# Seven-product units in two PSUM banks, with wider evictions and a moved first product

## The chip, the cores and the metric

The kernel runs on one core of a Trainium2 chip. The metric is the device time of one execution in microseconds (us); lower is better. TensorE is written PE, its weight loads PEld, VectorE DVE, ScalarE ACT, GpSimd POOL, and the queue that issues most of the DMAs SP.

## The reference, cut to what matters

The kernel computes a two-layer encoder for 512 tokens of width 1024. Each layer mixes retention and differential attention, and then adds a SwiGLU block. Only the last line of a layer is touched by the change:

```
for l in range(DEPTH):                       # 2
    ...
    x = x + jnp.concatenate([ret, da], axis=-1) @ w_out[l]
    h = rms_norm(x, ffn_norm_g[l])           # x: 512 x 1024
    x = x + (jax.nn.silu(h @ w_gate[l]) * (h @ w_up[l])) @ w_down[l]   # inner width 2816
```

## The kernel before, in words

Activations lie transposed: features on the 128 partitions, tokens along the free axis. A float32 product is made of three matmuls of a shortened format: each operand is split into a high part `hi` (a cast on ACT) and a rest `lo` (a subtraction on DVE), and hi\*hi, hi\*lo and lo\*hi are summed in PSUM.

The inner width of 2816 is 22 blocks of 128. The first 4 blocks go through ordinary products (`gate_up`). The other 18 use a seven-product scheme, one level of Strassen-Winograd: a "unit" takes the place of a 2x2 block product and makes seven products of half size instead of eight. There are 26 units in a layer: 18 for gate and up (n = 512, so that a product is 12 matmuls of 256 columns) and 2 x 4 for the way down (n = 384, 9 matmuls). I number them 0 to 25 in the order in which the program writes them: up units 0 to 5, up unit 6, down units 7 to 10, up units 11 to 15, up unit 16, down units 17 to 20, up units 21 to 25.

A unit is the generator `seven`. It loads four weight blocks (three DMAs on SP, and one on POOL that adds to what the first one brought), makes the sums of blocks that the scheme needs (L783, L785 on DVE), and splits three pairs of blocks into `hi` (L754, ACT) and `lo` (L755, DVE): pair a holds the weights of products b11 and t2, pair s31 those of t3 and t1, pair b those of b21 and t4; s4 is split alone for b22 (L748, L749). `hi` and `lo` have three buffers each (`NHL`), and a unit uses three, so pair a of a unit can be written only when the unit before has read its own pair a for the last time, in product t2. In the same way s31 waits for product t3 of the unit before, and pair b for t4.

The seven products go into PSUM. Four of them (b11, t2, t3, t4) pile up in one bank called `pa`, and the running sum is copied out between them: after b11 (L803), after t2 (L806) and after t3 (L809), on ACT each time, and after t4 inside `finish`. A product on `pa` has to wait until the copy ahead of it has read the bank. Product b21 has the bank `pb`, and t1 and b22 share the bank `pc`. The pools give two banks to each of the tags acc (for `pa`), sc (`pb`) and o (`pc`). What follows in `finish` is silu (L106, ACT), products on DVE, and the splits of the result for the way down.

The loop over the units sets the written order: `next(unit)`, `next(units[i + 1])`, `next(unit, None)`. So the loads, the splits and product b11 of the next unit stand where the second `yield` of a unit is. This is not yet the order on the engines: a scheduler that works on its own estimate of the times places each engine's instructions, mostly as written, but it lets later matmuls go ahead where it expects a wait. Each engine then runs its instructions strictly in that order and waits on semaphores.

Of the kernel before, what the change touches and what calls it, by code (L numbers as in the profile page):

```python
# [10 lines left out]
AF = mybir.ActivationFunctionType  # L11
ALU = mybir.AluOpType

P = 128
# [10 lines left out]
C = 256  # L25
# [29 lines left out]
def encoder_kernel(ctx: ExitStack, tc: tile.TileContext, xT, wfirst, wsingle, wvv, wout, wgu, wdn, wds, prm, lam, cst, outT):  # L55
    nc = tc.nc
# [10 lines left out]
    def nm(s):  # L67
        uid[0] += 1
        return f"{s}{uid[0]}"

    def big(s, dt=F32, tag="w", bufs=NW):
        return tpool.tile([P, T], dt, tag=tag, name=nm(s), bufs=bufs)
# [4 lines left out]
    def bank(tag, bufs):  # L77
        return psum.tile([P, 512], F32, tag=tag, name=nm(tag), bufs=bufs)

    acc_bank = lambda: bank("acc", 2)  # L80
    sc_bank = lambda: bank("sc", 2)
    out_bank = lambda: bank("o", 2)
# [98 lines left out]
    def pair():  # L181

        t = tpool.tile([P, 2, T], F32R, tag="h", name=nm("h"), bufs=8)
        return t[:, 0], t[:, 1]
# [25 lines left out]
    def cut(pair, *idx):  # L210
        return tuple(t[idx] for t in pair)
# [102 lines left out]
    def layer(l, n1, h, x_src, first_raw):  # L314
# [272 lines left out]
        q, k = [None] * 4, [None] * 4  # L587
# [50 lines left out]
        n2, h2, x = Norm(), [], []  # L638
# [73 lines left out]
        H1, H2 = slice(0, C), slice(C, T)  # L712
# [45 lines left out]
        def four(raw):  # L758
            return new_chunk(1024)[0] if raw else tpool.tile([P, 1024], F32, tag="ah", name=nm("s"), bufs=NAH)
# [3 lines left out]
        def seven(src, n, right, finish, by_load=True):  # L763


            A1, A2 = slice(0, n), slice(n, 2 * n)
            turns[0] += 1
            s31, a, b = (four(raw)[:, : 2 * n] for raw in (False, True, turns[0] % 2))
            s4 = big("s4")[:, :n]
            blocks = src.rearrange("p (i n) -> p i n", n=n)  # L770
            if by_load:
                sums = s31.rearrange("p (i n) -> p i n", n=n)
                nc.sync.dma_start(sums, blocks[:, 1:2].broadcast_to([P, 2, n]))
                nc.sync.dma_start(a[:, A1], blocks[:, 0])
                nc.sync.dma_start(b, src[:, 2 * n :])
                nc.gpsimd.dma_start(sums, blocks[:, 0::3], accum_op=ALU.add)  # L776
            else:
                nc.sync.dma_start(a, src[:, : 2 * n])
                nc.sync.dma_start(b, src[:, 2 * n :])
                i = nc.vector.tensor_tensor(s31[:, A2], a[:, A2], b[:, A2], op=ALU.add)  # L780
                tc.add_manual_dep(i.ins, last_split[0], order, reason="unit by unit")
                nc.vector.tensor_tensor(s31[:, A1], a[:, A2], a[:, A1], op=ALU.add)
            i = nc.vector.tensor_tensor(a[:, A2], a[:, A1], s31[:, A2], op=ALU.add)  # L783
            tc.add_manual_dep(i.ins, last_split[0], order, reason="unit by unit")
            nc.vector.tensor_tensor(s4, b[:, A1], a[:, A2], op=ALU.add)  # L785
            g1, s2 = split_in(a, n)
            first_cast[0] = last_cast[0]
            s3, s1 = split_in(s31, n)
            g2, u2 = split_in(b, n)
            s4 = cut(split_to(s4, [big("s4", F32R, "mix", NMIX)[:, :n] for _ in range(2)]), slice(None))  # L790

            pa, pb, pc = (bank() for bank in (acc_bank, sc_bank, out_bank))

            def product(ps, w, r, start):
                for k in range(n // P):
                    L, R = cut(w, slice(None), slice(k * P, (k + 1) * P)), right[k][r]
                    for i, (x1, x2) in enumerate(((0, 0), (0, 1), (1, 0))):
                        nc.tensor.matmul(ps[:, :C], L[x1], R[x2], start=start and k + i == 0, stop=k == n // P - 1 and i == 2, skip_group_check=True)  # L798


            g, u = big("g"), big("u")
            product(pa, g1, "b11", True)
            nc.scalar.copy(g[:, H1], pa[:, :C])  # L803
            yield
            product(pa, s2, "t2", False)
            nc.scalar.copy(g[:, H2], pa[:, :C])  # L806
            product(pc, s1, "t1", True)
            product(pa, s3, "t3", False)
            nc.scalar.activation(u[:, H2], pa[:, :C], AF.Copy, scale=-1.0)  # L809
            nc.vector.tensor_tensor(u[:, H2], u[:, H2], pc[:, :C], op=ALU.subtract)  # L810
            product(pb, g2, "b21", True)
            nc.vector.tensor_tensor(g[:, H1], pb[:, :C], g[:, H1], op=ALU.add)
            product(pa, u2, "t4", False)
            yield
            product(pc, s4, "b22", False)
            nc.vector.tensor_tensor(g[:, H2], pc[:, :C], g[:, H2], op=ALU.add)
            finish(g, u, pa[:, :C])

        def activation(act, j, pairs, wait):


            def finish(g, u, pa):
                tc.add_manual_dep(func(g, g, AF.Silu), first_cast[0], order, reason="the next unit first")
                if j < pairs:
                    u, half = big("u", tag="rn", bufs=4), u
                else:
                    half = u
                nc.vector.scalar_tensor_tensor(u[:, H1], pa, -1.0, g[:, H1], op0=ALU.mult, op1=ALU.mult)
                nc.vector.tensor_tensor(u[:, H2], half[:, H2], g[:, H2], op=ALU.mult)
                i = j % pairs  # L830
                spread = i == pairs - 1

                if j < pairs:
                    later.append(lambda: first_parts(u, spread))
                    if not (j == 0 and wait):
                        later.pop()()
                    return
                second_parts(u, act[i], spread)

            def first_parts(u, spread):  # L840
                t = big("b11", F32R, *(("rn", 4) if spread else ("w", NW)))
                t14 = pair()
                b11 = split_to(u[:, H1], (t[:, H1], t[:, H2]))
                nc.vector.tensor_tensor(u[:, H1], u[:, H1], u[:, H2], op=ALU.subtract)
                t1 = split_to(u[:, H1], cut(t14, slice(None), H1))
                act.append(dict(u=u, t14=t14, b11=b11, t1=t1))

            def second_parts(u, o, spread):
                v = o["u"]
                b2 = split_to(u, [big("b2", F32R, "mix", NMIX) for _ in range(2)] if spread else pair())  # L850
                nc.vector.scalar_tensor_tensor(v[:, H1], v[:, H1], -1.0, u[:, H2], op0=ALU.mult, op1=ALU.subtract)
                nc.vector.tensor_tensor(v[:, H2], u[:, H2], v[:, H2], op=ALU.subtract)
                t23 = split_to(v, pair())
                nc.vector.scalar_tensor_tensor(u[:, H1], v[:, H1], -1.0, u[:, H1], op0=ALU.mult, op1=ALU.subtract)
                t4 = split_to(u[:, H1], cut(o["t14"], slice(None), H2))
                for r, t, s in (("b21", b2, H1), ("b22", b2, H2), ("t2", t23, H1), ("t3", t23, H2)):
                    o[r] = cut(t, slice(None), s)
                o["t4"] = t4

            return finish  # L860

        def plain(act, j):
            def finish(g, u, pa):
                func(g, g, AF.Silu)
                nc.vector.scalar_tensor_tensor(u[:, H1], pa, -1.0, g[:, H1], op0=ALU.mult, op1=ALU.mult)
                nc.vector.tensor_tensor(u[:, H2], u[:, H2], g[:, H2], op=ALU.mult)
                act.append(split(u, *(("rn", 4) if j < 2 else ("h", 8))))

            return finish

        def down(m):
            def finish(g, u, pa):
                nc.vector.tensor_tensor(x[m], x[m], g, op=ALU.add)
                nc.vector.tensor_tensor(x[m + 4][:, H2], x[m + 4][:, H2], u[:, H2], op=ALU.add)
                nc.vector.tensor_tensor(x[m + 4][:, H1], x[m + 4][:, H1], pa, op=ALU.subtract)

            return finish

# [5 lines left out]
        act, n = [], a1 * P  # L884
# [4 lines left out]
        for m in range(KT):  # L889
# [6 lines left out]
            w = cut(ww, slice(None), slice(m % 2 * n, (m % 2 + 1) * n))  # L896
            ps = any_bank()
# [8 lines left out]
        for i, (a0, a1) in enumerate(FFN[1:]):  # L906
            act, half = [], (a1 - a0) // 2
# [20 lines left out]
        n, late = (a1 - a0) * P, []  # L928
        for m in range(KT):
            w = chunk(wdn[l, m][:, PLAIN * P :], n)  # L930
            if l + 1 == DEPTH and m == KT - 1:

                for t, queue in ((H1, nc.sync), (H2, nc.scalar)):
                    ps = any_bank()
# [5 lines left out]
            ps = any_bank()  # L940
# [17 lines left out]
    n, h, raws = Norm(), [], []  # L958
# [7 lines left out]
    for l in range(DEPTH):  # L966
        if l:
            raws = [load_chunk(wfirst[l, c]) for c in range(4)]
        n, h = layer(l, n, h, xT if l == 0 else xscr, raws)
# [94 lines left out]
```

## Time and profile before

| what | value |
| --- | --- |
| median of 3 runs | 1256.27 us (1254.27 to 1256.29) |
| span of the profiled execution, first to last instruction | 1252.7 us |
| what the median lies above that span | 3.6 us |
| granted TensorE clock | 1.000 |
| matmuls of the units (L798) | 4032 of 7954 |
| DVE busy, whole span | 1000.6 us (80%) |
| ACT busy, whole span | 724.5 us (58%) |

The page of the profile gives the span of the execution that was profiled; an own time of that execution beside it is not given, and the median of the runs is 3.6 us above the span. Matmuls are pipelined in the record: each is drawn 283 ns long, while the next one starts 120 ns later. So a PE that looks busy all the time may still lose time between the starts, and I read the starts. The two layers give nearly the same pattern, with the units from 339 to 598 us in the first and from 961 to 1220 us in the second.

### The profile page before, as it was taken

To read this page: it belongs to the slowest core of one execution; us is meant where nothing else is said; L and a number is where in the kernel's file an instruction comes from. 1 tells how busy PE (TensorE), PEld (TensorE's weight loads), DVE (VectorE), ACT (ScalarE), POOL (GpSimd) and SP (SyncE) were. 2 spreads that over 40 slices of the span, in tenths; PEclk is the share of its full clock that TensorE was granted. 3 is DMA by queue.
4 is the path that set the end of the run, shared out by engine and by line. 5 is a ranking of instruction groups with operands and counts; after the bars stand their busy time and mean duration, and the time that the engine had idled before them with its cause. 6 is when DMAs were issued, how large, how long until landed. Compare 5 with 4: busy or idle time off the path is not lost.

```text
span 1252.7 us, 20478 instructions
## 1 busy us (share of the span) xinstructions
PE 1235.7 (99%) x7954; PEld 1110.4 (89%) x7954; DVE 1000.6 (80%) x1742; ACT 724.5 (58%) x1230; POOL 80.7 (6%) x94
## 2 busy tenths in 40 slices
PE   9999999999999999999999999999999999999998
PEld 7888988788799999999888889987788999999997
DVE  6899769877978888886648997698779788888863
ACT  6778747455455555554538785564554565555541
POOL 1000000000011111110000000000100110110100
PEclk9999999999999999999999999999999999999999
DMA  7222213363176686683532122142632756866823
GB/s 260 84 68 68 68 67 120 100 151 101 54 171 156 155 220 158 156 220 89 170 104 85 51 84 68 51 151 76 159 101 64 179 148 170 211 150 169 207 69 101
DMA packets 67553, 157.81 MB, mean 126 GB/s; under 512 B 6144, under 2 KB 16640, under 8 KB 67456
## 3 DMA queue, kind: packets, MB, share of 16 engines
q1 hardware_dynamic: 52880, 130.90, 33.4%
q0 software_dynamic: 14144, 25.17, 12.0%
q8 instruction: 62, 1.02, 0.3%
q10 hardware_dynamic: 432, 0.44, 0.1%
q14 instruction: 35, 0.29, 0.1%
HBM read 152.29 MB, written 4.19 MB: 125 GB/s over the span
## 4 chain that ended last, share of the span: by engine, by line
PE 96%; DVE 2%; ACT 1%; DMA 0%; issue 0%; ACTq 0%
PE acc L798 22%; PE o L798 11%; PE acc L205 10%; PE acc L207 10%; PE acc L206 10%; PE sc L798 5%; PE o L205 3%; PE o L206 3%; PE o L207 3%; PE sc L205 3%; PE sc L207 3%; PE sc L206 3%; PE sc L404 2%; PE o L508 2%; PE sc L492 1%; PE aux L420 1%
## 5 line engine op out<-in xcount | busy, mean ns | idle before, releaser
L194 ACT CAST hi<-raw 128x1024 fp32r<-128x1024 f32 (+2 forms) x115 | 113.3, 992 | 122.3 <-PE sc L206 40.5
L198 DVE TENSOR_TENSOR lo<-raw,hi 128x1024 fp32r<-128x1024 f32 (+2 forms) x116 | 132.7, 1148 | 42.0 <-ACT hi L194 41.6
L205 PE MATMUL acc<-h,hi 128*128 128x512 f32 (+1 forms) x344 | 134.2, 392 | 1.1 <-ACT h L216 1.1
L207 PE MATMUL acc<-h,lo 128*128 128x512 f32 (+1 forms) x344 | 134.6, 391 | 0.0
L206 PE MATMUL acc<-h,hi 128*128 128x512 f32 (+1 forms) x344 | 134.5, 391 | 0.0
L798 PE MATMUL acc<-hi,hi 128*128 128x256 f32 x432 | 122.9, 284 | 0.0
L798 PE MATMUL acc<-hi,lo 128*128 128x256 f32 x432 | 122.2, 283 | 0.0
L798 PE MATMUL acc<-lo,hi 128*128 128x256 f32 x432 | 122.1, 283 | 0.0
L754 ACT CAST hi<-raw 128x1024 fp32r<-128x1024 f32 (+1 forms) x78 | 76.6, 982 | 76.4 <-PE acc L798 30.1
L754 ACT CAST hi<-s 128x1024 fp32r<-128x1024 f32 (+1 forms) x78 | 76.6, 982 | 62.2 <-issue 24.6
L755 DVE TENSOR_TENSOR lo<-s,hi 128x1024 fp32r<-128x1024 f32 (+1 forms) x78 | 89.0, 1141 | 20.9 <-ACT hi L754 20.4
L755 DVE TENSOR_TENSOR lo<-raw,hi 128x1024 fp32r<-128x1024 f32 (+1 forms) x78 | 88.9, 1140 | 20.7 <-ACT hi L754 20.6
L798 PEld LDWEIGHTS acc<-hi,hi 128*128 128x128 f32 x432 | 82.7, 191 | 0.4
L798 PEld LDWEIGHTS acc<-lo,hi 128*128 128x128 f32 x432 | 82.8, 192 | 0.2
L798 PEld LDWEIGHTS acc<-hi,lo 128*128 128x128 f32 x432 | 82.8, 192 | 0.0
L205 PEld LDWEIGHTS acc<-h,hi 128*128 128x128 f32 x344 | 64.6, 188 | 14.6 <-ACT h L216 1.3
L207 PEld LDWEIGHTS acc<-h,lo 128*128 128x128 f32 x344 | 64.6, 188 | 13.2 <-DVE lo L198 0.2
L206 PEld LDWEIGHTS acc<-h,hi 128*128 128x128 f32 x344 | 64.7, 188 | 12.8
L776 POOL DMA_DIRECT2D s<-in_wgu x36 | 43.5, 1208 | 445.6 <-DMA s<-in_wgu 262.7
L798 PE MATMUL o<-b,s 128*128 128x256 f32 x480 | 66.0, 283 | 0.0
L798 PEld LDWEIGHTS o<-b,s 128*128 128x128 f32 x480 | 61.4, 192 | 0.2
L106 ACT ACTIVATE sc<-sc,mx 128x512 f32<-128x512 f32 x64 | 46.0, 720 | 18.1 <-DVE mx L408 17.6
(267 smaller groups left out, 3709.5 us busy)
## 6 DMA issues: line engine op xcount, KB each, us to landing
s<-in_wgu SPq DMA_DIRECT2D x54, 512.0 KB, 5.9
s<-in_wgu POOLq DMA_DIRECT2D x36, 512.0 KB, 8.6
raw<-in_wgu SPq DMA_DIRECT2D x34, 512.0 KB, 4.8
raw<-in_wsingle SPq DMA_DIRECT2D x32, 512.0 KB, 3.7
raw<-in_wgu SPq DMA_DIRECT2D x36, 256.0 KB, 3.5
s<-in_wds SPq DMA_DIRECT2D x24, 384.0 KB, 3.6
raw<-in_wvv SPq DMA_DIRECT2D x16, 512.0 KB, 3.7
raw<-in_wout SPq DMA_DIRECT2D x16, 512.0 KB, 3.7
```

Source lines behind the costliest of these rows:

```text
L106: i = nc.scalar.activation(out, src, f, **kw).ins
L194: c = nc.scalar.copy(hi[:, s], raw[:, s])
L198: nc.vector.tensor_tensor(lo[:, s], raw[:, s], f32(hi[:, s]), op=ALU.subtract)
L205: first = nc.tensor.matmul(out, L[0], R[0], start=start, stop=False)
L206: nc.tensor.matmul(out, L[0], R[1], start=False, stop=False)
L207: nc.tensor.matmul(out, L[1], R[0], start=False, stop=stop)
L404: nc.tensor.matmul(ps, q[m][:, t], k[m][part], start=part == 0, stop=part == 1)
L508: i = nc.tensor.matmul(o[b, c * C : (c + 1) * C], v[pr // 2][2 * c + j][:, (pr % 2) * P + hh * HD : (pr % 2) * P + (hh + 1) * HD], s[c][:, ...
L754: last_cast[0] = nc.scalar.copy(hi, raw).ins.name
L755: last_split[0] = nc.vector.tensor_tensor(lo, raw, f32(hi), op=ALU.subtract).ins.name
L776: nc.gpsimd.dma_start(sums, blocks[:, 0::3], accum_op=ALU.add)
L798: nc.tensor.matmul(ps[:, :C], L[x1], R[x2], start=start and k + i == 0, stop=k == n // P - 1 and i == 2, skip_group_check=True)
```

## The change

A unit now takes two banks, `pa` (acc) and `px` (sc). The left half of `px` receives b21 and the right half t1 and b22, so that one operation over 512 columns adds both to `g`. The running sum after t1 is copied out by ACT (L808), the one after t3 is subtracted straight from the bank by DVE (L810), and the one after t4 is copied by ACT (L814). Behind that, `finish` has one multiplication over 512 columns instead of two over 256, and `down` two additions instead of three. The second `yield` moves up: loads, splits and b11 of the next unit now stand ahead of b21, t4 and b22 of a unit, where they stood ahead of b22 alone.

```diff
-            pa, pb, pc = (bank() for bank in (acc_bank, sc_bank, out_bank))
+            pa, px = acc_bank(), sc_bank()
...
-            product(pa, s2, "t2", False)
-            nc.scalar.copy(g[:, H2], pa[:, :C])
-            product(pc, s1, "t1", True)
-            product(pa, s3, "t3", False)
-            nc.scalar.activation(u[:, H2], pa[:, :C], AF.Copy, scale=-1.0)
-            nc.vector.tensor_tensor(u[:, H2], u[:, H2], pc[:, :C], op=ALU.subtract)
-            product(pb, g2, "b21", True)
-            nc.vector.tensor_tensor(g[:, H1], pb[:, :C], g[:, H1], op=ALU.add)
-            product(pa, u2, "t4", False)
-            yield
-            product(pc, s4, "b22", False)
-            nc.vector.tensor_tensor(g[:, H2], pc[:, :C], g[:, H2], op=ALU.add)
-            finish(g, u, pa[:, :C])
+            product(pa, H1, s2, "t2", False)
+            nc.scalar.copy(g[:, H2], pa[:, H1])
+            product(px, H2, s1, "t1", True)
+            nc.scalar.activation(u[:, H2], px[:, H2], AF.Copy, scale=-1.0)
+            product(pa, H1, s3, "t3", False)
+            nc.vector.tensor_tensor(u[:, H2], u[:, H2], pa[:, H1], op=ALU.subtract)
+            yield
+            product(px, H1, g2, "b21", False)
+            product(pa, H1, u2, "t4", False)
+            nc.scalar.activation(u[:, H1], pa[:, H1], AF.Copy, scale=-1.0)
+            product(px, H2, s4, "b22", False)
+            nc.vector.tensor_tensor(g, px, g, op=ALU.add)
+            finish(g, u)
...
-                nc.vector.scalar_tensor_tensor(u[:, H1], pa, -1.0, g[:, H1], op0=ALU.mult, op1=ALU.mult)
-                nc.vector.tensor_tensor(u[:, H2], half[:, H2], g[:, H2], op=ALU.mult)
+                part, u = u, big("u", tag="rn", bufs=4) if j < pairs else u
+                nc.vector.tensor_tensor(u, part, g, op=ALU.mult)
...
                 nc.vector.tensor_tensor(x[m], x[m], g, op=ALU.add)
-                nc.vector.tensor_tensor(x[m + 4][:, H2], x[m + 4][:, H2], u[:, H2], op=ALU.add)
-                nc.vector.tensor_tensor(x[m + 4][:, H1], x[m + 4][:, H1], pa, op=ALU.subtract)
+                nc.vector.tensor_tensor(x[m + 4], x[m + 4], u, op=ALU.add)
```

Three places show what becomes of the engines' orders. In a row, the name before the arrow is what is written, and the last name behind it is the weights; acc is `pa`. The first place is PE at down units 7 and 8. Before, acc922 is unit 7 and acc940 unit 8; the weights hi914 and lo915 are pair a of unit 7, hi932 pair a of unit 8, and hi916 pair s31 of unit 7.

```order
L798 MATMUL acc922_4475<-h909_4379,hi914_4459 128x256
L798 MATMUL acc922_4475<-h909_4379,lo915_4460 128x256
L798 MATMUL acc940_4582<-b11810_3708,hi932_4566 128x256 x2
L798 MATMUL acc922_4475<-h870_4108,hi916_4463 128x256 x2
L798 MATMUL acc922_4475<-h870_4108,lo917_4464 128x256
```

The same place now, with acc915 for unit 7, sc916 its second bank, acc932 for unit 8, hi924 pair a of unit 8, and hi911 pair b of unit 7:

```order
L798 MATMUL sc916_4438<-b2901_4361,s4913_4433 128x256
L798 MATMUL sc916_4438<-b2900_4360,s4914_4434 128x256
L798 MATMUL acc932_4548<-b11808_3705,hi924_4532 128x256 x2
L798 MATMUL acc915_4437<-h809_3706,hi911_4429 128x256 x2
L798 MATMUL acc915_4437<-h809_3706,lo912_4430 128x256
```

Before, b11 of unit 8 stands right behind the last matmuls of t2 of unit 7, whose buffer its weights need; now it stands behind b21 and b22 of unit 7, with t3, b21 and b22 in between.

The second place is PE at up unit 2, where t2 ends. Before (acc824; sc825 is its bank for b21):

```order
L798 MATMUL acc824_3805<-hi756_3426,hi816_3789 128x256
L798 MATMUL acc824_3805<-lo757_3427,hi816_3789 128x256
L798 MATMUL acc824_3805<-hi756_3426,lo817_3790 128x256
L798 MATMUL sc825_3806<-bh685_3153,hi820_3797 128x256
L798 MATMUL sc825_3806<-bl686_3154,hi820_3797 128x256
```

Now (acc822):

```order
L798 MATMUL acc822_3777<-hi756_3426,hi814_3761 128x256
L798 MATMUL acc822_3777<-lo757_3427,hi814_3761 128x256
L798 MATMUL acc822_3777<-hi756_3426,lo815_3762 128x256
L798 MATMUL acc822_3777<-hi690_3164,hi816_3765 128x256
L798 MATMUL acc822_3777<-lo691_3165,hi816_3765 128x256
```

Before, 14 matmuls (b21 of the unit, and the first two of the next unit) stood between t2 and t3 on the same bank; now t3 follows t2 on that bank with nothing between.

The third place is ACT at the first unit of the second way down, unit 17. Before, its first copy is L803 of g1111 (acc1108), and silu is that of units 15 (g1072) and 16 (g1091):

```order
L106 ACTIVATE g1072_5421<-g1072_5421 128x512
L754 CAST hi1102_5677<-s1096_5663 128x768
L809 ACTIVATE u1092_5557<-acc1088_5553 128x256
L748 CAST b21093_5587<-u1073_5422 128x512
L754 CAST hi1104_5681<-s1098_5665 128x768
L748 CAST h1095_5593<-u1035_5183 128x512
L803 COPY g1111_5692<-acc1108_5689 128x256
```

Now it is L803 of g1093 (acc1091), and g1074 is the silu of unit 16:

```order
L754 CAST hi1083_5615<-raw1080_5606 128x768
L748 CAST b21076_5554<-u1057_5367 128x512
L748 CAST h1078_5560<-u1021_5157 128x512
L748 CAST s41089_5627<-s41082_5608 128x384
L754 CAST hi1085_5619<-s1079_5605 128x768
L106 ACTIVATE g1074_5499<-g1074_5499 128x512
L803 COPY g1093_5633<-acc1091_5631 128x256
```

The silu of unit 16 now stands between the cast of pair s31 and the copy of b11 of unit 17; on PE, t2 of unit 17 follows its b11 with only two matmuls (of t1) between, where 21 stood before. On SP and POOL the DMAs of the units are issued in the same order as before.

More of the change, by code (lines that the diff above doesn't have):

```diff
@@ L790, in seven, with product @@
             s4 = cut(split_to(s4, [big("s4", F32R, "mix", NMIX)[:, :n] for _ in range(2)]), slice(None))
-            pa, pb, pc = (bank() for bank in (acc_bank, sc_bank, out_bank))
-            def product(ps, w, r, start):
+            pa, px = acc_bank(), sc_bank()
+            def product(ps, t, w, r, start):
                 for k in range(n // P):
@@ L797, in product @@
                     for i, (x1, x2) in enumerate(((0, 0), (0, 1), (1, 0))):
-                        nc.tensor.matmul(ps[:, :C], L[x1], R[x2], start=start and k + i == 0, stop=k == n // P - 1 and i == 2, skip_group_check=True)
+                        nc.tensor.matmul(ps[:, t], L[x1], R[x2], start=start and k + i == 0, stop=k == n // P - 1 and i == 2, skip_group_check=True)
             g, u = big("g"), big("u")
-            product(pa, g1, "b11", True)
-            nc.scalar.copy(g[:, H1], pa[:, :C])
+            product(pa, H1, g1, "b11", True)
@@ L804, in seven @@
+            nc.scalar.copy(g[:, H1], pa[:, H1])
             yield
-            product(pa, s2, "t2", False)
-            nc.scalar.copy(g[:, H2], pa[:, :C])
-            product(pc, s1, "t1", True)
-            product(pa, s3, "t3", False)
-            nc.scalar.activation(u[:, H2], pa[:, :C], AF.Copy, scale=-1.0)
-            nc.vector.tensor_tensor(u[:, H2], u[:, H2], pc[:, :C], op=ALU.subtract)
-            product(pb, g2, "b21", True)
-            nc.vector.tensor_tensor(g[:, H1], pb[:, :C], g[:, H1], op=ALU.add)
@@ L819, in activation, with finish @@
+            yield
+            product(px, H1, g2, "b21", False)
[4 more added lines that the diff above has]
+            finish(g, u)
         def activation(act, j, pairs, wait):
-            def finish(g, u, pa):
+            def finish(g, u):
                 tc.add_manual_dep(func(g, g, AF.Silu), first_cast[0], order, reason="the next unit first")
[L824 to L828, printed above, removed]
-                nc.vector.tensor_tensor(u[:, H2], half[:, H2], g[:, H2], op=ALU.mult)
+                part, u = u, big("u", tag="rn", bufs=4) if j < pairs else u
+                nc.vector.tensor_tensor(u, part, g, op=ALU.mult)
@@ L862, in plain, with finish @@
         def plain(act, j):
-            def finish(g, u, pa):
+            def finish(g, u):
                 func(g, g, AF.Silu)
-                nc.vector.scalar_tensor_tensor(u[:, H1], pa, -1.0, g[:, H1], op0=ALU.mult, op1=ALU.mult)
-                nc.vector.tensor_tensor(u[:, H2], u[:, H2], g[:, H2], op=ALU.mult)
+                nc.vector.tensor_tensor(u, u, g, op=ALU.mult)
                 act.append(split(u, *(("rn", 4) if j < 2 else ("h", 8))))
@@ L871, in down, with finish @@
         def down(m):
-            def finish(g, u, pa):
+            def finish(g, u):
                 nc.vector.tensor_tensor(x[m], x[m], g, op=ALU.add)
-                nc.vector.tensor_tensor(x[m + 4][:, H2], x[m + 4][:, H2], u[:, H2], op=ALU.add)
-                nc.vector.tensor_tensor(x[m + 4][:, H1], x[m + 4][:, H1], pa, op=ALU.subtract)
+                nc.vector.tensor_tensor(x[m + 4], x[m + 4], u, op=ALU.add)
             return finish
```

## Prediction

> **What bounds the kernel now.** I read the page's shares and its chain of waits first, then the two stages with units by windows, then what the units' line waits for, then single starts in the timeline.
>
> ```profile
> PE 1235.7 (99%) x7954; PEld 1110.4 (89%) x7954; DVE 1000.6 (80%) x1742; ACT 724.5 (58%) x1230; POOL 80.7 (6%) x94
> PE 96%; DVE 2%; ACT 1%; DMA 0%; issue 0%; ACTq 0%
> ```
>
> PE ends the chain nearly everywhere. The change adds and removes no matmul, so it can only move time that PE loses between matmuls. That time stands in the two stages (one for each layer; columns: length, then busy time of PE, PEld, DVE, ACT and POOL, clock, DMA share, GB/s):
>
> ```profile
> 339.00:600.00 261.00, 257.61 (x2067) 252.91 (x2068) 212.33 (x360) 141.53 (x239) 29.23 (x26) 1.00 0.66 162
> 961.00:1222.00 261.00, 257.31 (x2066) 252.49 (x2066) 211.85 (x360) 140.28 (x238) 27.68 (x23) 1.00 0.66 162
> ```
>
> Within the first, PE waits for these (its weight loads counted too, so that a wait can stand twice):
>
> ```profile
> L798 PE MATMUL acc<-bh,hi x72: 280/283/387, 339.1 to 581.1; 128*128 128x256 f32 x72
> L798 PE MATMUL o<-b,s x240: 274/283/283, 357.1 to 597.2; 128*128 128x256 f32 x120
> its engine sat idle before it (us, times) until:
>   ACT hi L754: 5.8, 10
>   DVE lo L755: 3.0, 4
>   DVE x L641: 0.6, 1
>   DVE u L828: 0.2, 1
> ```
>
> Nothing here names a copy out of PSUM (L803, L806, L809): what PE waits for is weights, that is the cast to `hi` and the subtraction to `lo`. How much it is shows in the starts, since a matmul of 256 columns follows the last one by 0.12 us, and one of 512 by 0.23:
>
> ```profile
> 392.82 0.28 PE L798 MATMUL acc<-hi,hi 128*128 128x256 f32 x1
> 392.94 0.28 PE L798 MATMUL acc<-lo,hi 128*128 128x256 f32 x1
> 393.06 0.28 PE L798 MATMUL acc<-hi,lo 128*128 128x256 f32 x1
> 393.99 0.39 PE L798 MATMUL acc<-bh,lo 128*128 128x256 f32 x1 [0.64 <-DVE lo L755]
> 394.21 0.28 PE L798 MATMUL acc<-bh,hi 128*128 128x256 f32 x1
> ...
> 1242.02 0.39 PE L206 MATMUL o<-h,hi 128*128 128x512 f32 x1
> 1242.24 0.39 PE L207 MATMUL o<-h,lo 128*128 128x512 f32 x1
> ```
>
> A stage holds 2016 unit matmuls x 0.120 = 241.9 us and 51 others x 0.227 = 11.6, together 253.5 of 261.0: 7.5 are lost, and 0.7 just ahead of it, 8.2 us a layer and 16.4 in all. Above, 393.06 to 393.99 loses 0.81, and the start after it another 0.10, which follows nearly every such wait.
>
> **The losses of before, by place** (sums of the starts that came late). At the start of the stage 1.5 us, below. At b11 of units 8 and 18 1.0 each, with 0.45 behind it: 2.9. At the `lo` of b11 of units 5 and 15 0.9 each: 1.8, the piece above. The other 2.0 are some dozen places where `hi` arrives just in time, 0.1 to 0.25 each.
>
> **What goes.** At unit 8:
>
> ```profile
> 420.96 0.28 PE L798 MATMUL acc<-h,hi 128*128 128x256 f32 x1
> 421.08 0.28 PE L798 MATMUL acc<-h,lo 128*128 128x256 f32 x1
> 421.32 0.83 ACT L754 CAST hi<-raw 128x768 fp32r<-128x768 f32 x1 [0.57 <-PE acc L798]
> 422.06 0.36 ACT L806 COPY g<-acc 128x256 f32<-128x256 f32 x1
> 422.20 0.51 PE L798 MATMUL acc<-b,hi 128*128 128x256 f32 x2 [0.85 <-ACT hi L754]
> ```
>
> The last reader of the buffer starts at 420.96 and ends at 421.24; the cast begins 0.08 later and takes 0.83; b11 starts 0.05 behind it. So a cast needs 0.24 + 0.83 + 0.05 = 1.1 us from where the last reader's slot ends, and with the 1.05 of 1024 columns (rows below) 1.35. The order now puts 27 matmuls there (t3, b21, b22), 3.2 us. All 2.9 go. For the rows that need durations:
>
> ```profile
> L754 ACT CAST hi<-s 128x1024 fp32r<-128x1024 f32 x27 | 28.3, 1048 | 18.7 <-PE acc L798 8.8 <-issue 7.0 <-ACT h L748 1.4
> L755 DVE TENSOR_TENSOR lo<-s,hi 128x1024 fp32r<-128x1024 f32 x27 | 33.0, 1223 | 7.3 <-ACT hi L754 7.2
> L106 ACT ACTIVATE g<-g 128x512 f32<-128x512 f32 x18 | 11.4, 633 | 20.2 <-DVE g L816 19.9
> L803 ACT COPY g<-acc 128x256 f32<-128x256 f32 x26 | 9.7, 372 | 11.8 <-PE acc L798 11.8
> L809 ACT ACTIVATE u<-acc 128x256 f32<-128x256 f32 x26 | 9.8, 378 | 0.0
> L810 DVE TENSOR_TENSOR u<-u,o 128x256 f32<-128x256 f32 x26 | 10.8, 414 | 0.0
> L816 DVE TENSOR_TENSOR g<-o,g 128x256 f32<-128x256 f32 x26 | 11.0, 425 | 13.9 <-PE o L798 13.7
> L828 DVE SCALAR_TENSOR_TENSOR u<-acc,g 128x256 f32<-128x256 f32 x12 | 5.0, 420 | 2.8 <-ACT g L106 2.8
> L873 DVE TENSOR_TENSOR x<-x,g 128x512 f32<-128x512 f32 x8 | 5.5, 690 | 0.2
> L783 DVE TENSOR_TENSOR raw<-raw,s 128x512 f32<-128x512 f32 x17 | 11.7, 686 | 0.8 <-DMA s<-in_wgu 0.8
> ```
>
> The `lo` of units 5 and 15 came late because the multiplication L828, ahead of it on DVE, waited for silu (the 2.8 of its row). In the new order the split stands behind subtractions and additions whose inputs are there by then, and its product has 4.6 us or more between the last reader and the first `lo`, where a cast and a split need 0.24 + 1.05 + 1.22 + 0.1 = 2.6. The 1.8 go.
>
> **Merged evictions.** For each unit, four DVE operations of 256 columns (4 x 0.42) become two of 512 (2 x 0.69, the row L873): 0.3 us less, 8 us of DVE in a layer; in `down` the counts are 5 to 3, with the same result. ACT gets one more copy of 0.38: 26 x 0.38 = 9.8 us on 141.5 of 261. Neither engine ends the chain, so both count nothing as long as PE has its weights; the cover is their idle 19% and 46%.
>
> **What comes.** A copy between two products on `pa` costs 0.24 (tail and start) + 0.37 + 0.05 = 0.66 us from the end of one to the start of the other, and 0.1 behind it where PE really waits. Going through the order with 0.12 a matmul, that room is too short at three places in a layer. Unit 2, t2 to t3: no room, 0.75. Unit 7, t2 to t3: two matmuls, 0.66 - 0.24 + 0.1 = 0.5. Unit 17, b11 to t2: two matmuls, and the copy stands behind the cast of s31 (free when t3 of unit 16 ends, 1.08 before b11's end) and silu: 0.24 + 0.83 + 0.63 + 0.37 + 0.05 = 2.1 against 1.08 + 0.24 = 1.3, so 0.8, less some 0.2 since ACT begins an operation before the last has ended, 0.65 with the tail. Together 1.9. Bounds: 1.2 (0.4 each, ACT free and no tail) and 4.4 (a whole cast more in front of each).
>
> The start of the stage:
>
> ```profile
> 339.31 0.28 PE L798 MATMUL acc<-bl,hi 128*128 128x256 f32 x1
> 339.43 0.34 PE L798 MATMUL o<-hi,hi 128*128 128x256 f32 x1
> 339.61 0.28 PE L798 MATMUL o<-lo,hi 128*128 128x256 f32 x1
> 340.16 0.50 PE L207 MATMUL acc<-hi,lo 128*128 128x512 f32 x1 [0.27 <-DVE lo L198]
> ```
>
> Two matmuls of t1 that shortened this wait for a `lo` now stand behind it: it grows by 0.3, 1.5 to 1.8.
>
> Arrivals just in time: pair s31 has 1.0 to 1.3 us at units 9, 11, 19 and 21 against 1.1 and 1.35, 0.15 to 0.2 each, and some four others cost 0.1: 1.05 where 2.0 were.
>
> **The moved step.** Unit by unit, four DMAs, the sums and the three splits come along with b11. SP and POOL issue in the same order, and from the freeing of a unit's buffers (t3 or t4 two or three units earlier) to its b11 lie as many matmuls as before, within 2.6 us. The one load that is late is that of unit 12 (0.8 in the row L783): 22.1 us of matmuls before and 22.3 now. I count 0; its b11 now has 1.2 us between the cast and its start, and without that it would cost up to 0.8.
>
> **An added wait.** t4 now waits for DVE's subtraction L810, where ACT's copy L809 freed the bank. Behind t4 on PE stand t1 and t2 of the next unit. With DVE free it needs 0.24 + 0.41 + 0.05 = 0.7, and nine units in a layer have 1.1 to 1.4 there: nothing. Behind a whole `lo` split it needs 1.9, and each loses 0.6: 5.4 a layer. Adding up the DVE queue by the rows above, the tightest is unit 5, where it leaves 0.3. I take 0.5 a layer, near the lower end, since at the other eight the queue in front is short operations.
>
> **The sum for a layer:** 8.2 before; now 1.8 + 1.05 + 1.9 + 0.5 = 5.25; 2.95 less, 5.9 for both. The span goes from 1252.7 to 1246.8, and with the 3.6 that the median of 1256.3 lies above it, 1250.4 us.
>
> **The rivals.** First, *DVE gates PE* (slower): the nine units above lose 0.6 each, 5.4 instead of 0.5: 1250.4 + 9.8 = 1260. It decides from 0.38 us a place, where the gain is gone. For it: DVE is busy 212 of 261 us and keeps strict order. Against it: with 0.3 us less a unit DVE has more room.
>
> Second, *the shared bank holds b21 up* (slower): b21 writes one half of `px` while ACT has to read t1 from the other half; if that counts as the same place, b21 waits for L808. t2 lies between, 1.08 or 1.44 us, and the copy needs 0.24 + 0.38 + 0.05 = 0.67: nothing. Behind a cast it needs 1.7 (1.5 in down units), 0.3 to 0.4 too much; if half of the 52 units meet that, 9 us, 1259. Against it: ACT is idle 46%, and where I followed its order the copy stands ahead of the next cast. The Trainium skill, in PSUM — Partial Sum Buffer, section PSUM bank collisions raise a hardware error, says to guard PSUM by bank (and quadrant), not by address, as two engines in one bank collide even in other columns. By that rule the wait exists, by the rows it is hidden; no run of before shows it, since no bank there was read while another half was due.
>
> Third, *the waits only move* (same): b11 needs its pair after t1 and t3 (2.9 us up, 2.2 down), where the written order had four products. With queues on ACT and DVE it might come 0.1 late in all 26 units, with nothing left of the gain: 3 us a layer, 1256. For it: the casts wait 8.8 us for PE already. Against it: the needs of 1.35 and 2.6 fit.
>
> Fourth, *more goes than I count*: the new waits and the arrivals cost half, 3 us less: 1247.
>
> **How the numbers follow.** A change within 0.2% (2.5 us) can hardly be told from none here. The forecast case (1247.5 to 1253.7) gets 0.56, the fourth rival 0.09, the third 0.20, DVE 0.11, the bank 0.04. That makes 0.65 faster, 0.20 same, 0.15 slower. The range takes in the forecast, the larger gain and the moved waits up to 1257; what is left out, both slower rivals and a still larger gain, holds under 0.2.
>
> **What would show it.** Right: no wait of 1 us at units 8 and 18, no late `lo` at units 5 and 15, new waits of PE for L806 at units 2 and 7 and for L803 at unit 17, DVE 4 to 8 us less busy in a stage and ACT 10 more. Wrong: PE waiting for L810 in many units, for L808 at b21, or for L754 at most b11.

## Result and the profile after

The changed kernel takes 1244.85 us (median of 4 runs, 1244.77 to 1246.83), the kernel before 1255.35 us beside it (1254.27 to 1256.29). The ratio is 0.9924, 95% interval 0.991 to 0.9938: faster by 0.8%. The forecast was 1250.4 us, 1246 to 1257. The sign was right. The gain was 9.5 to 10.5 us where 5.9 were forecast, and the time lies 1.2 us below the range.

Both kernels have two levels of time about 2 us apart (1254.3 and 1256.3; 1244.8 and 1246.8), which the last section follows up. On the lower level the gain is 9.5 us, and the profiled spans, 1252.7 and 1243.0, differ by 9.7.

From the page after, the engines and the chain; then the two stages by windows (length, busy PE, PEld, DVE, ACT, POOL, clock, DMA share, GB/s):

```profile
PE 1231.1 (99%) x7954; PEld 1109.9 (89%) x7954; DVE 989.3 (80%) x1638; ACT 739.3 (59%) x1282; POOL 80.6 (6%) x94
339.00:600.00 261.00, 259.29 (x2084) 255.09 (x2085) 207.11 (x309) 149.38 (x266) 29.23 (x26) 1.00 0.67 162
961.00:1222.00 261.00, 259.86 (x2088) 255.69 (x2087) 207.06 (x310) 149.52 (x265) 27.68 (x23) 1.00 0.68 166
```

PE does the same 7954 matmuls. In a stage DVE is 5 us less busy (4 to 8 were forecast) and ACT 8 to 9 more (10 were forecast). What PE waits for in the unit matmuls of the first stage:

```profile
its engine sat idle before it (us, times) until:
  ACT g L806: 1.8, 4
  ACT hi L754: 1.1, 2
  ACT g L803: 0.8, 2
  ACT u L808: 0.7, 3
  DVE x L641: 0.6, 1
```

Before, this list began with 5.8 us for casts and 3.0 us for `lo`. Now copies out of PSUM lead it, and `lo` is gone. At unit 8, where b11 waited 0.85 us for its cast, it follows at once; at unit 2, t3 now waits for the copy L806 (PE, then ACT):

```profile
422.46 0.52 PE L798 MATMUL sc<-b,s 128*128 128x256 f32 x3
422.82 0.40 PE L798 MATMUL acc<-b,hi 128*128 128x256 f32 x2
...
369.69 0.39 PE L798 MATMUL acc<-hi,hi 128*128 128x256 f32 x1 [0.46 <-ACT g L806]
369.91 0.28 PE L798 MATMUL acc<-lo,hi 128*128 128x256 f32 x1
...
369.26 0.37 ACT L806 COPY g<-acc 128x256 f32<-128x256 f32 x1 [1.67 <-PE acc L798]
```

I summed all starts of unit matmuls that came late (over 0.12 us behind the one ahead, or over 0.23 behind one of 512 columns). Before, 16.2 us over both layers; after, 7.7, or 3.8 a layer. That is 8.5 of the 9.7 us. (The expectations below have 4.15 a layer in place of 3.8: there the longer slots of the wider matmuls ahead of three starts still count as late.)

### The profile page after: what moved, and what is told of

It reads as the page before. It is cut to its first block, busy times and chain, and to the rows that moved or that the text cites. A ratio compares the mean times of both kernels' runs of the same rounds, so it can differ in the third digit from the quotient of the medians.

```text
span 1243.0 us, 20513 instructions
## 1 busy us (share of the span) xinstructions
PE 1231.1 (99%) x7954; PEld 1109.9 (89%) x7954; DVE 989.3 (80%) x1638; ACT 739.3 (59%) x1282; POOL 80.6 (6%) x94
## 5 line engine op out<-in xcount | busy, mean ns | idle before, releaser
L194 ACT CAST hi<-raw 128x1024 fp32r<-128x1024 f32 (+2 forms) x115 | 113.5, 993 | 117.5 <-PE sc L206 42.7
L798 PE MATMUL sc<-b,s 128*128 128x256 f32 x480 | 69.0, 283 | 0.0
L798 PEld LDWEIGHTS sc<-b,s 128*128 128x128 f32 x480 | 62.6, 192 | 0.0
```

The source lines that it names most:

```text
L194: c = nc.scalar.copy(hi[:, s], raw[:, s])
L798: nc.tensor.matmul(ps[:, t], L[x1], R[x2], start=start and k + i == 0, stop=k == n // P - 1 and i == 2, skip_group_check=True)
```

## The experiments

Twelve kernels ran, each beside the kernel before. Three theories stood at the start. A: the gain comes with the exchanged evictions (t1's sum copied by ACT, L808, and t3's subtracted by DVE, L810), which let the scheduler set b11 further from t2. B: it comes with the moved step. C: it comes with the wide operations, which relieve DVE.

| run | time, us (median) | ratio to before, 95% interval |
| --- | --- | --- |
| yield_only | 1254.3 | 0.9998 (0.9990 to 1.0007) |
| merge_only | 1246.5 | 0.9936 (0.9924 to 0.9949) |
| before_l810 | 1240.3 | 0.9886 (0.9873 to 0.9900) |
| silu_late | 1244.75 | 0.9922 (0.9908 to 0.9935) |
| t1_two | 1243.15 | 0.9909 (0.9896 to 0.9923) |
| parts_u12 | 1244.05 | 0.9918 (0.9905 to 0.9932) |
| b21_own_bank | 1243.75 | 0.9911 (0.9898 to 0.9925) |
| narrow | 1249.4 | 0.9958 (0.9946 to 0.9971) |
| after_old_copy | 1279.5 | 1.0196 (1.0182 to 1.0210) |
| l810_px | 1248.6 | 0.9956 (0.9943 to 0.9968) |
| l810_copy4 | 1245.3 | 0.9927 (0.9915 to 0.9940) |
| l810_copy4_yield | 1241.3 | 0.9898 (0.9884 to 0.9911) |

### The moved step alone: yield_only

```diff
+            yield
             product(pb, g2, "b21", True)
             nc.vector.tensor_tensor(g[:, H1], pb[:, :C], g[:, H1], op=ALU.add)
             product(pa, u2, "t4", False)
-            yield
```

> The kernel before with only the second yield moved ahead of b21: three banks and the old evictions stay. Theory A (the gain comes with the new evictions: the copy of t1 (L808) and the subtraction of t3 from its bank (L810) let the scheduler put b11 of the next unit further behind t2): PE's order stays that of before but for units 7 and 17, b11 of units 8 and 18 still follows t2 of units 7 and 17 at once and waits 1.0 us for its cast, the lo of units 5 and 15 is still 0.8 late, and the time is that of before within 1 us, 1253.5 to 1256. Theory B (the moved step is what brings the gain): those waits are gone and the time is 1245 to 1249.

Measured 1254.3, the kernel before to within 0.1%. The waits of PE in the first stage are those of before to the last digit, and b11 of unit 8 is as late:

```profile
  ACT hi L754: 5.8, 10
  DVE lo L755: 3.0, 4
...
422.20 0.50 PE L798 MATMUL acc<-b,hi 128*128 128x256 f32 x2 [0.85 <-ACT hi L754]
```

B is out for the old order: PE runs b11 where it ran it before. Between the last matmul of t2 and the first of the next unit's b11 stand as many matmuls as before at every unit of the first layer, none at units 7 and 17.

### Everything but the moved step: merge_only

```diff
-            yield
             product(px, H1, g2, "b21", False)
             product(pa, H1, u2, "t4", False)
             nc.scalar.activation(u[:, H1], pa[:, H1], AF.Copy, scale=-1.0)
+            yield
             product(px, H2, s4, "b22", False)
```

> The changed kernel with the second yield back in its old place (behind the copy of t4, ahead of b22): two banks and the wide evictions stay. Theory A (new evictions): nearly all of the gain stays. In the order b11 of unit 3 now follows t2 of unit 2 with nothing between (a cast of 1024 columns, 1.35 us, is late), t2 of unit 7 follows its b11 with two matmuls between (0.5), as at unit 17; against the changed kernel that is 1.4 + 0.5 more and 0.72 + 0.49 less at t3 of units 2 and 7, so 0.7 a layer more: 1246.2, 1245 to 1248. Theory B (moved step): most of the gain is gone, 1251 to 1255.

Measured 1246.5: some 8 of the 9.5 us come without the moved step. New against the changed kernel is the wait that the order had shown, b11 of unit 3 right behind t2 of unit 2:

```profile
370.31 0.39 PE L798 MATMUL acc<-bh,hi 128*128 128x256 f32 x1 [1.06 <-ACT hi L754]
```

### The exchanged evictions alone: before_l810

```diff
             product(pc, s1, "t1", True)
+            nc.scalar.activation(u[:, H2], pc[:, :C], AF.Copy, scale=-1.0)
             product(pa, s3, "t3", False)
-            nc.scalar.activation(u[:, H2], pa[:, :C], AF.Copy, scale=-1.0)
-            nc.vector.tensor_tensor(u[:, H2], u[:, H2], pc[:, :C], op=ALU.subtract)
+            nc.vector.tensor_tensor(u[:, H2], u[:, H2], pa[:, :C], op=ALU.subtract)
```

> The kernel before with only two evictions exchanged: t1 is copied out by ACT as soon as it is complete, and DVE subtracts t3 straight from its bank; three banks, narrow evictions and the old yield stay. Theory A (new evictions): these two lines alone bring the new order: between t2 and the next unit's b11 there are 1.9 us or more everywhere, between products on pa 0.8 or more, so that the late casts at units 8 and 18 go and no copy is late as at units 2, 7 and 17 of the changed kernel. What is left a layer is the start (1.0), arrivals just in time (1.0) and some 0.2 at t4: 2.2 against 4.15, so 3.9 less than the changed kernel: 1241, 1239.5 to 1243. Theory C (the wide evictions that relieve DVE are needed): lo stays late as at units 5 and 15 of before, 1.8 a layer, and the time is 1244.5 or more. Theory B (moved step): 1252 to 1256.

Measured 1240.3: 14 us faster than before and 4.5 us faster than the whole change. The waits of PE in the first stage:

```profile
its engine sat idle before it (us, times) until:
  ACT hi L754: 1.0, 1
  DVE x L641: 0.6, 1
  DVE u L810: 0.5, 2
  DVE lo L755: 0.2, 1
```

No copy L803 or L806 is in the list, and late starts sum to 3.0 us over both layers (before 16.2, changed kernel 7.7). The order shows why: between t2 and the next unit's b11 stand at least 16 matmuls everywhere, which is 1.9 us against the 1.1 to 1.35 that a cast needs; before there were none at units 7 and 17, and 10 to 12 at six others. The two lines were only exchanged together; what each is worth alone was not tried. From its page:

```profile
PE 1228.7 (99%) x7954; PEld 1109.5 (90%) x7954; DVE 999.1 (81%) x1742; ACT 725.6 (59%) x1230; POOL 80.7 (7%) x94
```

DVE runs all its narrow operations here, as many and as long as before (1000.6), and the late `lo` of units 5 and 15 are gone all the same: C's reason does not hold either.

### The exchange undone in the changed kernel: after_old_copy

```diff
             product(px, H2, s1, "t1", True)
-            nc.scalar.activation(u[:, H2], px[:, H2], AF.Copy, scale=-1.0)
             product(pa, H1, s3, "t3", False)
-            nc.vector.tensor_tensor(u[:, H2], u[:, H2], pa[:, H1], op=ALU.subtract)
+            nc.scalar.activation(u[:, H2], pa[:, H1], AF.Copy, scale=-1.0)
+            nc.vector.tensor_tensor(u[:, H2], u[:, H2], px[:, H2], op=ALU.subtract)
```

> The changed kernel with one exchange undone: t3's sum is copied out of pa by ACT again and t1 is subtracted from its bank by DVE, behind t3. Two banks, wide evictions, L814 and the moved step stay. Theory A (the copy of t1 and the subtraction of t3 bring the gain): the order gets bad again. By its rooms a layer loses 0.56 + 6 x 0.76 at t3 right behind t2 (units 0, 7, 11, 12, 17, 21, 22), 1.45 at b11 of unit 1 (a cast of 1024 columns, right behind t2 of unit 0), 4 x 0.26 at t4 and 4 x 1.0 at t1 (cast of s31, 0.2 us behind t3) of units 11, 12, 21 and 22, with the start 12.6 in place of 4.15: slower than the kernel before, 1262, 1256 to 1268. If the two banks or the wide evictions bring the gain: 1244 to 1248.

Measured 1279.5, slower than before by 2%. The sign and most places were right, the size was not: late starts sum to 40.6 us, not 25.

```profile
  DVE lo L755: 11.1, 25
  ACT hi L754: 10.7, 15
  ACT g L806: 7.0, 12
```

The rooms gave the copies and the casts, but I left out `lo`: b11 that stands close behind its cast waits again at its third matmul, 0.28 to 0.79 us in thirteen units of the first layer. The four corners now stand: neither 1254.3, the exchange alone 1240.3, the rest alone 1279.5, both 1244.85. The exchange is worth 14 us without the rest and 35 with it, and the rest costs 4.5 us with the exchange and 25 without.

### What the rest costs: l810_px, l810_copy4, l810_copy4_yield

Each starts from before_l810. The first puts b21 and t1/b22 into halves of one bank; the second copies t4 out by ACT; the third is the second with the moved step. The diff shows the main lines; besides, in the first b21 no longer opens its bank (`False` in place of `True`), and in the second and third the last multiplications and additions read the copy in `u` in place of `pa`.

```diff
l810_px
-            pa, pb, pc = (bank() for bank in (acc_bank, sc_bank, out_bank))
+            pa, px = acc_bank(), sc_bank()
+            pb, pc = px[:, H1], px[:, H2]
l810_copy4
             product(pa, u2, "t4", False)
+            nc.scalar.activation(u[:, H1], pa[:, :C], AF.Copy, scale=-1.0)
```

> The kernel before with t1's copy and t3's subtraction exchanged as in the run before_l810, and besides b21 and t1/b22 in the two halves of one bank; narrow evictions, no L814, the old yield. It isolates the shared bank. Theory A: b21 may now start only behind the copy of t1, the scheduler puts other matmuls there, and b11 of units 3, 4 and 5 comes right behind t2 of the unit before (0.0, 0.1 and 0.2 us against the 1.35 of a cast): 4.2 a layer more than before_l810, 1248.7, 1246.5 to 1251. If the shared bank costs nothing by itself: 1240.3.

Measured 1248.6, as the rooms gave it. PE's only long waits in the first stage are casts, at b11 of units 3, 4 and 5 (1.22, 1.10 and 0.98 us late):

```profile
  ACT hi L754: 7.4, 8
  DVE x L641: 0.6, 1
```

> The run before_l810 and besides the copy of t4 out of pa by ACT (L814) in place of DVE's reading of pa in the last step; three banks, narrow evictions, the old yield. By its rooms t2 of unit 16 has only two matmuls behind b11 (0.5), b11 of unit 13 1.2 us behind t2 of unit 12 (0.25), t1 of unit 7 0.8 us behind t3 of unit 6 (0.4): 3.1 a layer instead of 1.95, 1242.6 (1241 to 1244.5). If the early release of pa is worth something by itself: 1239.5 or less.

Measured 1245.3, spread over 1244.1 to 1246.5, later than expected. The rooms came out about as written; what they can't show is a load. In both layers unit 22's sum waited for its DMA, and its cast and b11 behind it (DVE, ACT, PE; here the first layer):

```profile
543.69 0.69 DVE L783 TENSOR_TENSOR raw<-raw,s 128x512 f32<-128x512 f32 x1 [3.31 <-DMA s<-in_wgu]
544.55 1.04 ACT L754 CAST hi<-raw 128x1024 fp32r<-128x1024 f32 x1 [4.00 <-PE sc L798]
545.65 0.39 PE L798 MATMUL acc<-bh,hi 128*128 128x256 f32 x1 [1.21 <-ACT hi L754]
```

This wait is 3.5 of the 8.5 us of late starts. The DMA on POOL that adds to this load went out at 538.16, and what it waited for last, by the profile, was DVE; the second row is the same DMA in the next run:

```profile
538.16 1.20 POOL L776 DMA_DIRECT2D s<-in_wgu  x1 [4.62 <-DVE g L817]
535.30 1.20 POOL L776 DMA_DIRECT2D s<-in_wgu  x1 [3.52 <-DVE g L817]
```

> The run l810_copy4 with the second yield moved up as in the change: what then differs from the run b21_own_bank (1243.75) is only the width of the evictions. The two late t2 and b11 of units 16 and 13 go by the order, t1 of units 7 and 17 is 0.8 us behind t3 (0.4 each): 2.8 a layer, 1242 (1240.5 to 1243.5). If the moved step matters in this order: over 1 us from l810_copy4, either way.

Measured 1241.3, 4 us less than without the moved step. The wait at unit 22 is gone, with the DMA 2.9 us earlier (2.0 against PE's own progress), and late starts sum to 3.2 us against 8.5. So the moved step is worth nothing in the old order, 4 us in this one, and 1.7 in the changed kernel (merge_only). The same run bears on the width: b21_own_bank below differs from it by its wide operations alone, and takes 2.4 us more.

### The bank, the width and three small terms

> The changed kernel with three banks: b21 has a bank of its own, t1 and b22 share px, and g is completed by two subtractions or additions of 256 columns instead of one of 512; the moved step, L808, L810 and L814 stay. If a bank that two products share holds b21 up: no b21 starts right at the end of L808 any more, and its late starts at units 1 and 12 (0.25 and 0.43) are gone. The order changes with it: t2 follows b11 with two matmuls between at units 7, 15 and 17 (0.5 each), the shortage between t2 and t3 at units 2 and 7 is gone, and b21 of units 7 and 17 has only 0.8 us behind t4 of the unit before against a cast that needs 1.1 (0.4 each). In sum about 4 us a layer as in the changed kernel: 1244.5, 1243 to 1246.5. If the two banks were what made the order good, it is 1250 or more.

In the changed kernel, `pa, px, pb = acc_bank(), sc_bank(), out_bank()`, b21 goes into `pb`, and `g` is completed in two halves. Measured 1243.75. The waits of PE in the first stage:

```profile
  ACT g L803: 2.0, 6
  ACT hi L754: 1.0, 1
  DVE x L641: 0.6, 1
```

L808 is no longer among them; L803 is, at units 7, 15 and 17, as expected. In the changed kernel the shared bank, with the wide addition that it allows, thus costs 1.1 us, against 8.3 for the bank on top of the exchange alone.

> The changed kernel with two exchanges on ACT in each layer: the cast L748 of the result of unit 11 stands behind the copy L808 of unit 12, not ahead of it (and a silu behind one copy). PE's order is the same. If b21 of unit 12 starts late (0.33 and 0.10) because it writes the bank from which L808 still has to read t1, and L808 stands behind a cast that waits for DVE: the wait goes, 0.43 a layer, 1244.0 (1243.8 to 1244.3). If b21 waits for its weights or for something else, the time is that of the changed kernel.

```diff
+                        todo = later.pop()
+                        soon.append(todo) if wait and j == 1 else todo()
-                        later.pop()()
```

(`soon` is emptied behind the next unit's t3.) Measured 1244.05, 0.8 us less. In the changed kernel (two rows) b21 starts 0.05 us behind the end of L808, which stands behind a cast that waited for DVE; in the run (two rows) L808 is done early and b21 follows t2 at once:

```profile
461.22 0.38 ACT L808 ACTIVATE u<-sc 128x256 f32<-128x256 f32 x1
461.65 0.39 PE L798 MATMUL sc<-bh,hi 128*128 128x256 f32 x1 [0.17 <-ACT u L808]
...
460.17 0.38 ACT L808 ACTIVATE u<-sc 128x256 f32<-128x256 f32 x1 [0.60 <-PE sc L798]
461.41 0.28 PE L798 MATMUL sc<-bh,hi 128*128 128x256 f32 x1
```

So b21 does wait for the reader of the other half of its bank. The Trainium skill, PSUM — Partial Sum Buffer, section PSUM bank collisions raise a hardware error, has this as a rule: guard by bank, not by address. The program keeps to it, and the trace agrees: of 52 units, no b21 starts less than 0.05 us after L808's end, and four start right there, 0.05 us behind it.

> The changed kernel with each operation of 512 columns on DVE behind a unit (g, u times g, x plus u) cut into two of 256: banks, copies and the moved step stay. DVE has 0.3 us more a unit, 8 in a stage. If DVE is covered, only the order changes (t2 behind b11 with two matmuls between at units 6 and 18, 0.5 each, instead of units 7 and 17; t3 right behind t2 at unit 2 as now): 1244.8 within 1 us. If the relief of DVE is what keeps lo in time, lo is late again as in the kernel before, 0.8 to 0.9 at two units or more, and the time is 1247 to 1250.

Measured 1249.4, 4.5 us slower. Yet `lo` is late nowhere:

```profile
  ACT g L803: 2.9, 9
  ACT g L806: 1.1, 2
  ACT hi L754: 0.7, 4
  ACT u L808: 0.6, 2
```

Late starts sum to 11.1 us against 7.7: copies L803 at units 6, 7, 16 and 17 lose 0.5 us each (I had counted units 6 and 18 only; of such places the changed kernel has unit 17), and some starts lose 0.2 each. Another 1.3 us is lost behind the last units. PE's order is another one, and the width acts through it, not through DVE's load: here narrow operations cost 4.5 us, and between b21_own_bank and l810_copy4_yield they gain 2.4. The outcome of 1247 to 1250 that I gave to C was met by another mechanism than C's.

> The changed kernel with t1 of units 2 and 7 cut in two: its last two thirds of a down unit, or last half of an up unit (6 matmuls, 0.72 us), are held behind t2, so that six matmuls stand between t2 and t3 on the same bank where none and two stood. If what PE loses there (0.62 and 0.39, with 0.10 behind each) is the copy L806 between the two products, both waits go: 1.2 us a layer, 2.4 in all, 1242.4 (1242 to 1243). If the copy is late for another reason (ACT busy with casts), the waits stay or move to t2, and the time is 1244.2 to 1245.5.

```diff
+            some = turn in (2, 7)
+            cut1 = n // P - 2 if some else 0
+            if some:
+                product(px, H2, s1, "t1", True, range(cut1))
             t2 = product(pa, H1, s2, "t2", False)
             nc.scalar.copy(g[:, H2], pa[:, H1])
+            product(px, H2, s1, "t1", not some, range(cut1, n // P), t2 if some else None)
```

Measured 1243.15 with a spread of 1242.6 to 1243.4 on the lower level, 1.4 to 2.2 us less. Both waits for L806 are gone; 0.3 us a layer came back as b21 of unit 2 waiting for the copy of t1, which now ends later. The expected 2.4 missed that.

> The changed kernel with one pair of instructions exchanged on ACT in each layer: the copy L803 of b11 of unit 17 stands ahead of the silu of unit 16. If t2 of unit 17 waits 0.54 us because the copy stands behind the silu (0.63 long) and the cast ahead of it: the copy can start behind the cast, the wait falls to 0.1 or less, and the kernel is 0.8 to 1.1 us faster over both layers, 1243.9. If it is the short room alone (two matmuls, 0.24, against 0.66) 0.4 to 0.5 stay and the time is that of the changed kernel within 0.2 us.

Measured 1244.75: no gain. With the copy ahead of the silu t2 of unit 17 still starts 0.39 us late instead of 0.44. Changed kernel, then the run:

```profile
507.23 0.63 ACT L106 ACTIVATE g<-g 128x512 f32<-128x512 f32 x1
507.76 0.35 ACT L803 COPY g<-acc 128x256 f32<-128x256 f32 x1
508.17 0.50 PE L798 MATMUL acc<-h,hi 128*128 128x256 f32 x2 [0.28 <-ACT g L803]
...
507.80 0.37 ACT L803 COPY g<-acc 128x256 f32<-128x256 f32 x1 [0.36 <-PE acc L798]
508.23 0.51 PE L798 MATMUL acc<-h,hi 128*128 128x256 f32 x2 [0.23 <-ACT g L803]
```

The copy waits 0.36 us for PE itself: the room of two matmuls is too short, and the silu had ended in time.

## Why the prediction was right or wrong

**Right: the mechanism and the places.** The casts at units 8 and 18 and the `lo` of units 5 and 15 went. The new waits stand at the three places named: t3 of unit 2 lost 0.72 (forecast 0.75), t3 of unit 7 0.49 (0.5), t2 of unit 17 0.54 (0.65). The wait for a `lo` at the start of the stage grew by 0.30 a layer (0.3). The moved step counted 0, and alone it is 0; inside the change it is worth 1.7 (merge_only), which the forecast did not see. The second reason given for unit 17, the silu ahead of the copy, was wrong: silu_late shows the short room alone, so that this 0.65 came near by luck.

**Wrong: the size.** The measured time is 5.55 us below the forecast. What failed is the sum, in four terms, which make that up to within 0.2.

- *The 3.6 that the median lies above the span.* It is 1.8. The profiled execution ran on the lower level, and the median of the three runs shown lay on the upper one; the runs later put the kernel before at 1254.3. That is 1.75 us. Without it the forecast would have been 1248.6, and the same range moved with it (1244.25 to 1255.25) would have held the result.
- *The sums of late starts in the stages*, 2.0 us in both layers. Before, the places where a weight arrives just in time lose 2.4 a layer (2.1 and 2.7), where I had 2.0. After, of the 1.05 for them only 0.49 were left, the 0.5 for t4 behind L810 is 0.1, and the start lost 0.9 instead of 1.1. Against these stands what I had at nothing, b21 behind L808: 0.25 at unit 1 and 0.43 at unit 12.
- *The ends of the stages*, which the sum put at nothing: what follows the last unit is 0.7 us shorter in each layer, 1.4. Before, three weight loads there waited for the casts L194 (0.26, 0.44 and 0.44 us). In before_l810 and merge_only those waits are gone too; in narrow, b21_own_bank and the three runs on top of before_l810 they are there. They go with the order, not with one edit.
- *The rest*, 0.6: 0.2 us ahead of the first unit and 0.35 behind the last matmul.

**The rivals.** *DVE gates PE* did not occur: t4 is late at two units in a layer, by 0.04 and 0.06. (In before_l810 it is, once a layer, by 0.3.) *The shared bank* holds b21 up, which had been named as a sign of being wrong, but at two units in a layer and not at half of them: 1.4 us in all, not 9. *The waits only move* is out: 16.2 to 7.7. *More goes than I count* had the right sign and a chance of 0.09, too little: of its two halves the arrivals did cost half (0.49 for 1.05), the new waits did not (1.75 for 1.9).

**Not asked.** The prediction costed the order as it stood and did not ask which edit made it. The runs do: two lines, the exchange of L808 and L810. Why the scheduler's estimate then sets b11 further back was not traced. Of the rest, the bank (8 us alone on top of the exchange) and the copy L814 (5 us, 3.5 of them a late load) each cost time, and the moved step buys some of it back.

## What to carry to other kernels

Where a scheduler fixes the order, an edit is worth what it does to the order: print the matmuls that stand between a buffer's last reader and its next use, and price each room against the copy, the cast or the split that has to fit. That count put the waits where they later stood; it is blind to loads and to `lo` behind a cast. And before keeping a change of several parts, run each part alone: here two lines of it are 4.5 us faster than the whole.

## What the runs showed of the hardware

The two levels are PE's first microseconds, as far as two traces can show it. Matmuls of 512 columns at the start, where the programs are alike, in the changed kernel (lower level) and then in l810_px (profiled on the upper level, 1250.6 against 1248.6 in its other runs):

```profile
7.61 0.40 PE L206 MATMUL acc<-h,hi 128*128 128x512 f32 x1
7.85 0.39 PE L207 MATMUL acc<-h,lo 128*128 128x512 f32 x1
...
8.48 0.63 PE L206 MATMUL acc<-h,hi 128*128 128x512 f32 x1
8.91 0.63 PE L207 MATMUL acc<-h,lo 128*128 128x512 f32 x1
```

They follow each other by 0.23 us in the one and by 0.43 in the other, until 10.6 us; from there both run alike, 1.85 us apart. The granted clock reads 1.00 in this stretch in both. The Trainium skill, TensorE: Matmul & The Clock Gate, section Part 1: The HAM clock gate, says that PE starts at half rate and that the moment of release hangs on a window that runs freely, so that it differs from run to run. The two starts agree with the half rate (0.43 against 0.23 us); that such a window sets the moment, and why there are two levels only, no run here shows. For a kernel whose changes are worth 2 us, the level must be known on both sides before a median is set against a span.
